# Adding 19 small, unused loads to a tuned softmax

## The chip, the cores and the metric

One core of a Trainium2 chip. The metric is device time in microseconds (us). A transfer is issued when an engine's queue starts it, and has landed when its last byte is reported. DVE is VectorE, ACT is ScalarE, POOL is GpSimd, SP is SyncE. "c0" to "c7" are the eight chunks of the work.

## The reference

```
x: (16, 1024, 512) float32
x_scaled = x / 0.5
exp_x = exp(x_scaled - max(x_scaled, axis=-1))
return exp_x / sum(exp_x, axis=-1)
```

It is a softmax over rows of 512, at temperature 0.5. The kernel reads 33.55 MB and writes 33.55 MB.

## The kernel before

The rows are cut into eight chunks of 128 partitions x 16 rows x 512 (4 MB each) in six buffers; c6 and c7 reuse the buffers of c0 and c1. DVE finds the maxima and multiplies by the reciprocals, ACT takes the exponentials. Loads are issued from Sync's queue. Stores are issued from ACT's queue, in the middle of ACT's own work.

```python
    def load(c):
        if c < BUFS:                                   # BUFS = 6
            chunks[c] = data.tile([P, G, D], fp32, name="xt")
        else:
            chunks[c] = chunks[c - BUFS]
        xt = chunks[c]
        for lo, hi in LOADS[c]:
            nc.sync.dma_start(out=xt[:, lo:hi, :], in_=xr[c][:, lo:hi, :])
    ...
    def store(i):
        ...
                nc.scalar.dma_start(
                    out=outr[c][:, lo:hi, :], in_=chunks[c][:, lo:hi, :]
                )

    shift(0)                         # maxima (DVE); loads the chunk first
    shift(1)
    exponentials(0)                  # ACT
    for i in range(n):
        if i + 1 < n:
            exponentials(i + 1)
        scale_vector(i)              # reciprocal, multiply (DVE)
        scale_scalar(i)              # the last rows of the chunk (ACT)
        if i + 2 < n:
            shift(i + 2)
        store(i)
```

Semaphores are not in this source; the framework deals them out. The built program and the semaphore events of the trace show how: the 17 DMAs issued from Sync and ACT take eight completion semaphores in turn, A to H. A DMA that takes one over is made to wait until the DMA that had it last has landed. The order, with the landing in us in the trace of before:

| semaphore | first use | second use | third use |
|---|---|---|---|
| A | load c0, first part (5.6) | store c1 (88.6) | store c7 (159.7) |
| B | load c0, rest (12.9) | load c6 (95.0) | |
| C | load c1 (22.6) | load c7 (115.0) | |
| D | load c2 (32.3) | store c2 (108.0) | |
| E | load c3 (42.4) | store c3 (121.1) | |
| F | store c0 (69.3) | store c4 (130.7) | |
| G | load c4 (56.3) | store c5 (140.4) | |
| H | load c5 (75.6) | store c6 (150.1) | |

Every second user is due long after its predecessor has landed. The store of c3, for instance, is issued at 92.3 and inherits E from a load that landed at 42.4.

## Time and profile before

The time is 162.5 us (2 runs, 162.26 and 162.73).

| of the 160.6 us span | before |
|---|---|
| DVE busy | 134.6 us |
| ACT busy | 102.1 us |
| DMA moved | 67.13 MB, mean 418 GB/s |
| last store issued, landed | 147.55, 159.71 us |

The page of the kernel before, its busy times and the two lower rows of the 40 slices (a digit is tenths of a slice; DMA is the mean over the 16 DMA engines):

```profile
DVE 134.6 (84%) x45; ACT 102.1 (64%) x273; POOL 0.2 (0%) x4
...
DMA  5999999999999999999999999999999999999993
GB/s 182 471 400 506 400 400 498 408 392 484 424 400 384 400 457 449 400 441 465 400 424 473 408 408 492 400 392 498 416 392 490 424 392 457 457 392 449 465 392 139
```

The DMA engines are full from the second slice to the last but one. The view of waits of the kernel before, with engine and line, what it waited for, us in total, times, longest:

```profile
ACT xt L85 <- DVE bias L78: 41.2, 10, 5.9
DVE negmax L74 <- DMA xt<-in_x_dram: 9.5, 2, 4.8
DVE recip L100 <- ACT xt L85: 1.8, 1, 1.8
```

DVE waits for the first loads and then hardly ever. ACT waits for DVE. So ACT has slack, while DVE and the DMA engines have nearly none. The timeline of the kernel before, around the store of c3 (start, duration, engine, line; in square brackets the engine's idle time before and what ended it; other lines of the same stretch are left out, here and in the timelines below):

```profile
92.27 0.34 ACTq L119 DMA_DIRECT2D out_dram<-xt  x1
96.25 0.72 ACT L85 ACTIVATE xt<-xt,bias 128x512 f32<-128x512 f32 x1 [4.01 <-DVE bias L78]
108.89 0.34 ACTq L119 DMA_DIRECT2D out_dram<-xt  x1
112.74 0.24 DVE L100 RECIPROCAL recip<-sums 128x16 f32<-128x16 f32 x1
```

The store of c3 goes out at 92.27. The exponentials of c5 start at 96.25, when DVE delivers their bias. They end near 107.5, and DVE takes the reciprocal of their sums at 112.74. ACT is thus some 5 us ahead of DVE here.

### The profile page before, as it was taken

How to read it: one execution, taken by the hardware profiler on the slowest of the kernel's cores; microseconds unless marked ns; L12 is line 12 of the kernel's file. 1: busy time of each engine (PE TensorE's matmuls, PEld its weight loads, DVE VectorE, ACT ScalarE, POOL GpSimd, SP SyncE). 2: the span in 40 equal slices, each digit the busy share in tenths (PEclk: the TensorE clock that was granted, in tenths of full speed). 3: DMA queues.
4: the chain of work that ended last, by engine and by line, in shares of the span. 5: the costliest groups of instructions: out<-in, count | busy, mean ns of one | idle time of the engine just before them, and what ended most of it. 6: DMA issues, size and time to landing. Idle time of an engine off the chain costs nothing.

```text
span 160.6 us, 402 instructions
## 1 busy us (share of the span) xinstructions
DVE 134.6 (84%) x45; ACT 102.1 (64%) x273; POOL 0.2 (0%) x4
## 2 busy tenths in 40 slices
DVE  0507999999999999999999999999999999957000
ACT  3071549069979963998199909991899891790000
POOL 0000000000000000000000000000000000000000
DMA  5999999999999999999999999999999999999993
GB/s 182 471 400 506 400 400 498 408 392 484 424 400 384 400 457 449 400 441 465 400 424 473 408 408 492 400 392 498 416 392 490 424 392 457 457 392 449 465 392 139
DMA packets 2450, 67.13 MB, mean 418 GB/s; under 512 B 272, under 2 KB 272, under 8 KB 272
## 3 DMA queue, kind: packets, MB, share of 16 engines
q1 hardware_dynamic: 1296, 33.56, 49.3%
q10 hardware_dynamic: 1152, 33.55, 48.4%
q14 instruction: 2, 0.02, 0.0%
HBM read 33.55 MB, written 33.55 MB: 418 GB/s over the span
## 4 chain that ended last, share of the span: by engine, by line
DVE 80%; DMA 7%; ACT 4%; issue 0%; SPq 0%
DVE negmax L74 42%; DVE xt L102 36%; DMA xt<-in_x_dram 7%; ACT xt L85 4%; DVE bias L78 1%; DVE recip L100 1%; SPq L66 0%
## 5 line engine op out<-in xcount | busy, mean ns | idle before, releaser
L85 ACT ACTIVATE xt<-xt,bias 128x512 f32<-128x512 f32 x128 | 90.4, 708 | 41.7 <-DVE bias L78 41.2
L74 DVE TENSOR_REDUCE negmax<-xt 128x16 f32<-128x8192 f32 (+2 forms) x11 | 69.9, 6352 | 9.5 <-DMA xt<-in_x_dram 9.5
L102 DVE TENSOR_TENSOR xt<-xt,recip 128x7168 f32<-128x7168 f32 (+2 forms) x11 | 62.0, 5637 | 0.4
L85 ACT ACTIVATION_READ_ACCUMULATOR xt<-xt,bias 128x1 f32 x128 | 23.9, 187 | 0.0
L111 ACT ACTIVATE xt<-xt,recip 128x512 f32<-128x512 f32 x15 | 9.9, 706 | 0.0
L100 DVE RECIPROCAL recip<-sums 128x16 f32<-128x16 f32 (+2 forms) x11 | 2.4, 218 | 1.8 <-ACT xt L85 1.8
L78 DVE TENSOR_SCALAR bias<-negmax 128x16 f32<-128x16 f32 (+2 forms) x11 | 1.9, 173 | 0.4
L52 ACT ACT_TABLE_LOAD x1 | 1.3, 1283 | 0.7 <-PEq L148 0.7
L51 DVE MEMSET warm<- 128x1 f32 x1 | 0.1, 59 | 0.8 <-PEq L148 0.8
L52 ACT ACTIVATE warm<-warm 128x1 f32<-128x1 f32 x1 | 0.2, 203 | 0.0
L148 POOL MEMSET const-bfloat16-1.0<- 128x1 bf16 x1 | 0.1, 103 | 0.0
L148 POOL MEMSET const-uint8-127<- 128x1 uint8 x1 | 0.1, 103 | 0.0
L148 POOL MEMSET const-float32-1.0<- 128x1 f32 x1 | 0.1, 100 | 0.0
L148 POOL MEMSET const-float32-0.0<- 128x1 f32 x1 | 0.1, 99 | 0.2 <-issue 0.2
## 6 DMA issues: line engine op xcount, KB each, us to landing
out_dram<-xt ACTq DMA_DIRECT2D x8, 4096.0 KB, 22.8
xt<-in_x_dram SPq DMA_DIRECT2D x7, 4096.0 KB, 30.2
xt<-in_x_dram SPq DMA_DIRECT2D x1, 3072.0 KB, 11.7
xt<-in_x_dram SPq DMA_DIRECT2D x1, 1024.0 KB, 4.9
```

The lines of the kernel that those rows point to most:

```text
L51: nc.vector.memset(warm, 0.0)
L52: nc.scalar.activation(out=warm, in_=warm, func=EXP)
L74: nc.vector.tensor_reduce(negmax[:, 0:b], chunks[c][:, lo:hi, :], axis=AX, op=MAX, negate=True)
L78: nc.vector.tensor_scalar_mul(biases[i][:, 0:b], negmax[:, 0:b], 2.0)
L85: nc.scalar.activation(out=row, in_=row, func=EXP, bias=biases[i][:, g : g + 1], scale=2.0, accum_out=sums[i][:, g : g + 1],)
L100: nc.vector.reciprocal(recips[i][:, 0:b], sums[i][:, 0:b])
L102: nc.vector.tensor_mul(rows, rows, recips[i][:, 0:k].unsqueeze(2).broadcast_to((P, k, D)))
L111: nc.scalar.activation(out=row, in_=row, func=COPY, scale=recips[i][:, g : g + 1])
L148: nc = _bacc.Bacc("TRN2", target_bir_lowering=False, num_devices=1)
```

## The change

The added loads mark points in the program: their sizes are recognisable in the DMA records. Nothing reads what they load. The whole change, with its blank lines left out:

```diff
         xt = chunks[c]
+        if c in (3, 4, 5, 6):
+            mark_pool()
         for lo, hi in LOADS[c]:
             nc.sync.dma_start(out=xt[:, lo:hi, :], in_=xr[c][:, lo:hi, :])
+        if c == 7:
+            mark()
+    junk = stats.tile([16, D], fp32, name="junk", bufs=1)
+    junk2 = stats.tile([16, D], fp32, name="junk2", bufs=1)
+    def mark():
+        for n in range(14, 1, -2):
+            nc.sync.dma_start(
+                out=junk[0:n, 0 : 512 - 4 * n], in_=xr[0][0:n, 0, 0 : 512 - 4 * n]
+            )
+    def mark_pool():
+        for n in (2, 3, 11):
+            nc.gpsimd.dma_start(
+                out=junk2[0:n, 0 : 442 - 4 * n], in_=xr[0][0:n, 0, 0 : 442 - 4 * n]
+            )
```

## The prediction

> **What bounds the kernel now.** The busy table gives DVE 134.6 us (84%) and ACT 102.1 us (64%) of a 160.6 us span. The DMA row reads 9 in every slice but the first and the last: 67.1 MB at a mean of 418 GB/s. The chain of waits starts with the first load (11.7 us), then runs on DVE without a gap from 12.9 to 147.5 us; the last store is issued at 147.6 and lands at 159.7. So DVE and the DMA engines are both nearly full. ACT has slack: it sits idle 41.2 us behind DVE's bias, but every store is issued from ACT's queue, so whatever makes a store wait holds back the exponentials behind it.
>
> **What is added.** 12 loads on GpSimd's queue (4 times 2, 3 and 11 partitions) and 7 on Sync's (14, 12 ... 2 partitions), 120 rows of under 2 KB, together under 0.25 MB. At the measured 309 ns per 8 KB packet, a row costs (estimate) about 0.1 us of one engine: under 1 us per engine in all. Nothing reads them. Each overwrites the one before, so each waits for its landing, but on queues with nothing behind them. By work alone: +0.2 us.
>
> **What I think matters instead.** The trace's semaphore events show that the 17 DMAs from Sync and ACT take eight completion semaphores in turn; the ninth takes the first one's again. The Trainium skill, "DMA: Bandwidth & Descriptors", section "Why a DMA increments its semaphore by 16 and not by 1", says that two DMAs in flight on one semaphore can't be told apart. So I expect each DMA to be made to wait for the one eight places before. Before, that one has always long landed. Seven extra Sync DMAs after the last load use up nearly a whole round of the eight. I assume the order: last load (c7), store of c2, the seven marks, store of c3. Then the store of c3 takes the semaphore of the store of c2, its direct predecessor.
>
> **Cost.** The c2 store is issued at 75.7 and lands at 108.0 (it shares the engines with loads). The c3 store is issued at 92.3 now; it would wait until 108.0, with ACT behind it. The exponentials of c5 now run from 96.2 (bias ready) to 107.5 and would run 108.4 to 119.8. DVE's reciprocal of c5, now at 112.8, would start at 120.0: 7.1 us late. The exponentials of c6 then end at about 132.9, adding 0.6 us. The final store is issued 7.7 us later and lands 7.7 us later (12.1 us alone). The marks themselves land behind the c7 load, from about 115 us on, some 3 us apart, before the stores that reuse their semaphores are due.
>
> **Prediction.** 162.5 + 7.7 + 0.2 = about 170.4 us, 4.9% slower; range 166 to 175. Chances: faster 0.01, same 0.15, slower 0.84.
>
> **What would show it.** Waits of ACT: one hold of about 12 us ahead of the c5 exponentials, ended by the landing of the c2 store; DVE with one new gap of about 7 us near 113 to 120 us; the c3 store issued near 108; one or two DMA slices below 9 near the end; the GpSimd loads landing in a few us each, at no cost.
>
> **What would make it wrong.** If the marks fall elsewhere in the order: all seven before the c2 store makes that store wait for the c7 load, and ACT stops for 26 us (about 181 us); six before the c3 store makes it wait for the c7 load (about 174); marks spread wider leave at most a few us. If the semaphores aren't shared that way, it stays at 162.7. GpSimd's descriptor work could delay DVE or the first load; I give that little weight.

## The result, and the profile after

The time is 169.76 us (2 runs, 169.75 and 169.78), 4.5% slower: the ratio is 1.0447, with a 95% interval of 1.0382 to 1.0512. Ratios here are the record's, over the fast runs of the same rounds, so not quite the ratios of the medians that are quoted. Executions over 1.5% slower than the fastest of the same kernel are left out of the means.

The page of the changed kernel (same rows as before):

```profile
DVE 134.8 (80%) x45; ACT 102.1 (61%) x273; POOL 6.6 (4%) x16
...
DMA  5998999999899999999989899999589388988885
GB/s 189 442 495 374 488 391 468 407 429 435 383 375 485 390 464 414 422 445 399 476 383 495 382 484 390 484 383 417 240 375 503 130 375 374 499 374 375 374 374 250
```

The work of DVE and ACT is the same to 0.2 us. What is new is idle time of the DMA engines in the last third: slices of 240 and 130 GB/s, where every slice before, first and last aside, had at least 384. Its view of waits:

```profile
POOL junk L85 <- DMA junk<-in_x_dram: 76.1, 11, 8.4
ACT xt L106 <- DVE bias L99: 32.5, 8, 5.9
ACT xt L106 <- DMA out_dram<-xt: 16.7, 1, 16.7
DVE recip L121 <- ACT xt L106: 9.9, 3, 7.5
```

ACT has one wait that was not there, 16.7 us, ended by the landing of a store. DVE, which hardly waited for ACT before, now does for 9.9 us. POOL waits 76.1 us for its own loads, one after the other, and nobody waits for POOL. The timeline of the changed kernel at the same place:

```profile
89.38 0.33 SPq L68 DMA_DIRECT2D xt<-in_x_dram  x1
89.75 33.13 SPq L79 DMA_DIRECT2D junk<-in_x_dram  x4
108.58 0.34 ACTq L140 DMA_DIRECT2D out_dram<-xt  x1
109.02 0.72 ACT L106 ACTIVATE xt<-xt,bias 128x512 f32<-128x512 f32 x1 [16.66 <-DMA out_dram<-xt]
120.44 0.25 DVE L121 RECIPROCAL recip<-sums 128x16 f32<-128x16 f32 x1 [7.48 <-ACT xt L106]
121.66 0.34 ACTq L140 DMA_DIRECT2D out_dram<-xt  x1
```

The store of c3 goes out at 108.58 instead of 92.27. By the semaphore events the store of c2 had landed at 108.48. The exponentials of c5 start 12.8 us later than before; DVE's reciprocal of c5, 7.7 us later. The chain of work that ended last, followed back by the profile, now runs through that wait (start, duration, what):

```profile
75.78 32.70 DMA out_dram<-xt
108.58 0.34 ACTq L140
109.02 7.92 ACT xt L106 x23
```

The semaphores in the built program, from the last load on, are now:

| semaphore | was | now |
|---|---|---|
| C | load c7 | load c7 |
| D | store c2 | store c2 |
| E, F, G, H | store c3, c4, c5, c6 | Sync's loads of 14, 12, 10, 8 rows |
| A, B, C | store c7 (A) | Sync's loads of 6, 4, 2 rows |
| D | | **store c3, which has to wait for store c2** |
| E, F, G, H | | store c4, c5, c6, c7 |

### The profile page after: what moved, and what is told of

It is laid out like the page before. It is cut to its first block, busy times and chain, and to the rows that moved or that the text cites. A ratio compares the mean times of both kernels' runs of the same rounds, so it can differ in the third digit from the quotient of the medians.

```text
span 168.0 us, 429 instructions
## 1 busy us (share of the span) xinstructions
DVE 134.8 (80%) x45; ACT 102.1 (61%) x273; POOL 6.6 (4%) x16
## 4 chain that ended last, share of the span: by engine, by line
DVE 40%; DMA 26%; ACT 24%; issue 1%; ACTq 0%; SPq 0%
ACT xt L106 23%; DVE negmax L95 22%; DMA out_dram<-xt 19%; DVE xt L123 16%; DMA xt<-in_x_dram 7%; ACT xt L132 1%; DVE bias L99 1%; DVE recip L121 1%; ACTq L140 0%; SPq L68 0%; ACTq L106 0%
## 5 line engine op out<-in xcount | busy, mean ns | idle before, releaser
L85 POOL DMA_DIRECT2D junk<-in_x_dram x12 | 6.4, 531 | 76.9 <-DMA junk<-in_x_dram 76.1
```

The source lines that it names most:

```text
L85: nc.gpsimd.dma_start(out=junk2[0:n, 0 : 442 - 4 * n], in_=xr[0][0:n, 0, 0 : 442 - 4 * n])
```

## The experiments

The theory: the seven Sync loads take seven of the eight semaphores, so the c3 store takes over that of the store just ahead of it. ACT, which has to issue that store, stops until then, and DVE runs out of exponentials. The rivals: A, the GpSimd loads cost the time; B, the chain of Sync loads that wait for one another does; C, a cost for each load or packet.

Each result gives the median, the range and the kernel before of the same chip and rounds. All kernels computed the right result.

### pool_only: without Sync's loads

```diff
-        if c == 7:
-            mark()
```

> The change without its seven Sync loads; the twelve GpSimd loads stay. Theory (the c3 store is held by the semaphore it shares with the c2 store): the semaphores are dealt as before, the c3 store is issued near 92.3 us, time 162.5 to 162.9 us. Rival A (the GpSimd loads cost the time, by their descriptor work beside DVE or in the DMA engines): most of the 7 us stay, 167 us or more.

Measured: 163.80 us (163.57 to 163.81) against 162.28; ratio 1.0088 (1.0071 to 1.0105). The c3 store was issued at 92.24. DVE is busy for 134.6 us as before and the second part of c0 lands at 12.83 (12.86), so GpSimd's 6.3 us of issuing delays neither. So rival A falls as the main cause. But the GpSimd loads cost 1.4 us (by the ratio) where I expected at most 0.4; the last three runs take that up.

### sync_only: without GpSimd's loads

```diff
-        if c in (3, 4, 5, 6):
-            mark_pool()
```

> The change without its twelve GpSimd loads; the seven Sync loads stay. Theory: all of the loss stays, 169.4 to 169.9 us, the c3 store issued near 108.5 us. Rival A: back to 162.5 to 163 us. Both together: in between.

Measured: 169.33 us (168.98 to 169.78) against 162.28; ratio 1.0435 (1.0413 to 1.0457). The c3 store was issued at 107.86, right after the c2 store landed at 107.76. The time is just below the expected range. The seven Sync loads alone make nearly all of the loss. The two parts do not add up: 7.1 us and 1.4 us alone, 7.3 us together (by the ratios; own_rows, next, has both and shows 7.4 us with a narrower interval).

### own_rows: Sync's loads need not wait for each other

```diff
-    junk = stats.tile([16, D], fp32, name="junk", bufs=1)
+    junk = stats.tile([56, D], fp32, name="junk", bufs=1)
...
-                out=junk[0:n, 0 : 512 - 4 * n], in_=xr[0][0:n, 0, 0 : 512 - 4 * n]
+                out=junk[at : at + n, 0 : 512 - 4 * n],
+                in_=xr[0][0:n, 0, 0 : 512 - 4 * n],
             )
+            at += n
```

> As changed, but each of the seven Sync loads writes partitions of its own, so they need not wait for one another; the order of the semaphores stays. Theory: unchanged at 169.3 to 170 us, the c3 store still issued near 108.5 us. Rival B (the chain of loads that wait for one another stands in the way, on Sync's queue or at the end): faster by several us, towards 163.

Measured: 169.72 us (169.68 to 169.86) against 162.28; ratio 1.0459 (1.0444 to 1.0475). In the change the seven loads land one after the other, from 112.3 to 136.0 us. Here six have landed by 113.4, so that chain is gone (the seventh, at 118.4, had to wait for semaphore C, from the c7 load). The time is the same and the c3 store still goes out at 108.66. Rival B falls.

### hold_c3_only: the wait without any load

```diff
             if hi == end:
+                if c == 3:
+                    nc.scalar.activation(
+                        out=chunks[2][0:1, 0, 0:1], in_=warm[0:1, 0:1], func=COPY
+                    )
                 nc.scalar.dma_start(
```

This is the kernel before. The added instruction writes one element of c2's buffer and so has to wait until the store of c2 has read it and landed. The result stays right, as the store has already gone.

> The kernel before, with no added load at all; ahead of the c3 store ACT writes one element of c2's buffer, which has to wait for the landing of the c2 store. Theory: that hold alone makes the loss, 169.3 to 170.2 us, the c3 store issued near 108.5 us, DVE idle some 7 us ahead of the reciprocal of c5. Rivals A and B, and any cost of small packets in the engines: 162.5 to 163 us.

Measured: 169.28 us (169.16 to 169.33) against 162.28; ratio 1.0429 (1.0414 to 1.0445). The time is 0.02 us under the expected range. Its timeline:

```profile
107.94 0.20 ACT L121 ACTIVATE xt<-warm 1x1 f32<-1x1 f32 x1 [15.75 <-DMA out_dram<-xt]
108.00 0.34 ACTq L124 DMA_DIRECT2D out_dram<-xt  x1
108.44 0.72 ACT L85 ACTIVATE xt<-xt,bias 128x512 f32<-128x512 f32 x1 [0.30 <-issue]
119.86 0.25 DVE L100 RECIPROCAL recip<-sums 128x16 f32<-128x16 f32 x1 [7.08 <-ACT xt L85]
```

This is the pattern of the changed kernel, with no extra load in the program: ACT stops 15.75 us for the c2 store, and DVE then stops 7.08 us for ACT. The hold alone gives 7.0 us, of the 7.1 us that the seven Sync loads cost. The late store's own traffic is not what costs: the last store but one has landed (155.00) before the last is issued (155.41), so nothing queues at the end, and the last is late because DVE was. This is the strongest of the runs.

### sync_marks4, sync_marks5, sync_marks6, sync_marks8: other numbers of loads

If the number of loads decides which landing the c3 store inherits, the cost should jump up and down with it. If each load has a price, it should grow evenly.

```diff
-        for n in range(14, 1, -2):
+        for n in range(14, 7, -2):     # 4; 5 and 6 likewise; 8: range(16, 1, -2)
```

> As changed, with four Sync loads (14 to 8 partitions) instead of seven. By the built program the c3 store now takes over the semaphore of the c1 store (lands at 88.6 us in the trace of before), the c4 store that of the c6 load (95.0), the c5 store that of the c7 load (115.0): all before they are due (92.3, 108.9, 125.5). Theory: 162.5 to 162.9 us. Rival C (a cost that grows with the number of loads, one us each): 166.7 us.

> Five Sync loads. The c3 store takes over the semaphore of the c6 load (lands 95 to 96 us): held 3 to 4 us, inside ACT's wait for the bias of c5 (96.2). The c4 store takes over that of the c7 load (115.0), due at 108.9: held 6 us, of which ACT's slack takes about 4.5. Theory: 163 to 165 us, best guess 164.2. Rival C: 167.7 us.

> Six Sync loads, one fewer than in the change. The c3 store takes over the semaphore of the c7 load, which lands near 112 us without the c3 store's traffic. Theory: slower than with seven loads: the c3 store issued near 112.2 us, 3.6 us later than with seven, time 172.8 to 174 us. Rival C: faster than with seven, 168.7 us.

> Eight Sync loads (one of 16 partitions first). The c3 store takes over the semaphore of the first of these loads, which lands right behind the c7 load, near 112.3 us. Theory: 172.8 to 174.2 us, the c3 store issued near 112.4 us. Rival C: 170.8 us.

| Sync loads | c3 store inherits from | c3 store issued | time, us (range) | before | ratio |
|---|---|---|---|---|---|
| 0 (pool_only) | load c3 | 92.24 | 163.80 (163.57 to 163.81) | 162.28 | 1.0088 |
| 4 | store c1 | 92.42 | 164.13 (164.04 to 164.27) | 162.58 | 1.0108 |
| 5 | load c6 | 96.42 | 164.61 (164.08 to 164.71) | 162.58 | 1.0129 |
| 6 | load c7 | 112.27 | 173.45 (173.36 to 173.59) | 162.58 | 1.0681 |
| 7 (change) | store c2 | 108.58 | 169.76 (169.75 to 169.78) | 162.50 | 1.0447 |
| 8 | first Sync load | 112.51 | 174.04 (173.80 to 174.14) | 162.58 | 1.0715 |

Six loads are 3.7 us slower than seven, and one more than five costs 9 us. Rival C, an even price, falls. The issue times of the c3 store were forecast to half a microsecond. The times with 5, 6 and 8 loads fell into the expected ranges; with 4 the time came out 1.2 us above it, near pool_only: these kernels all carry the GpSimd loads, whose cost I had left out.

Five loads show how much is forgiven. The c3 store waits until 96.42, which ACT would have spent waiting for the bias of c5 anyway. The c4 store waits for the c7 load and goes out at 116.47 instead of 108.89. The view of waits of sync_marks5 shows this second hold and what DVE lost:

```profile
ACT xt L106 <- DMA xt<-in_x_dram: 7.4, 1, 7.4
DVE recip L121 <- ACT xt L106: 4.8, 2, 3.0
```

DVE loses 3.0 us more than before, and the last store is issued 3.2 us later, at 150.75. Yet it lands only 1.2 us later than in pool_only (161.85 against 160.69). When compute is on time the last store queues behind the one ahead of it: in the kernel before it is issued at 147.55 while its predecessor lands at 150.06. A delay of the computation first uses up that queue.

### marks_on_gpsimd: all 19 loads, but from GpSimd

```diff
     def mark():
         for n in range(14, 1, -2):
-            nc.sync.dma_start(
+            nc.gpsimd.dma_start(
```

> All nineteen loads stay, with their sizes, places and the waits among themselves; the seven of Sync are issued from GpSimd's queue instead, which by the built program has semaphores of its own. Theory: the stores' semaphores are dealt as before, the c3 store is issued near 92.3 us, 162.5 to 163.0 us. Rival (the loads' work or packets cost the time, whoever issues them): 169 to 170 us.

Measured: 164.48 us (164.41 to 164.66) against 162.36; ratio 1.0130 (1.0113 to 1.0147). The c3 store was issued at 92.24. The same loads of the same sizes, issued where they take none of the stores' semaphores, cost 2.1 us instead of 7.3. The semaphores were forecast correctly, but the time was 1.5 us too low, again for the small loads' own cost.

### pool_4x16, pool_12x16, pool_12x1: what the small loads cost by themselves

In pool_only every instruction of DVE and ACT is where it was: the last store is issued at 147.52 (before 147.55). But its last engine finishes at 160.69 instead of 159.71, and its first at 158.77 instead of 158.49. After that, Sync goes through eight waits, some 60 ns each by the trace, before its drain instruction. Call what comes after the last landing the close: to the drain it takes 0.51 us, where before it took 0.12. So the 1.4 us are about 1.0 us in the DMA engines and 0.5 us at the close. The number of semaphores is not what sets this: in the runs with twelve GpSimd loads Sync waits for A to H in this order, and only what stands from the last store's semaphore on is left after its landing. That takes 0.51 us where the last store has A (0 and 8 Sync loads), 0.26 with E (4), 0.20 with F (5), 0.14 with G (6) and 0.08 with H (7, the change). In the kernel before the last store has A too, but there the wait for A stands second to last. The question was how the 1.0 us comes about. All three edits change the GpSimd loads of pool_only alone:

```diff
-        for n in (2, 3, 11):           # pool_4x16: for n in (11,):
-                out=junk2[0:n, 0 : 442 - 4 * n], in_=xr[0][0:n, 0, 0 : 442 - 4 * n]
+                out=junk2[0:16, 0 : 442 - 4 * n],      # pool_4x16 and pool_12x16
+                in_=xr[0][0:16, 0, 0 : 442 - 4 * n],   # pool_12x1: 0:1 in both
```

> What the twelve GpSimd loads cost: alone they cost 1.4 us where 0.2 was predicted (163.8 us; the last store lands 1.0 us later, its first engine only 0.3 us later). Here each trio of 2, 3 and 11 rows is one load of 16 rows of 1592 B: the same 64 rows in 4 loads, one row of each for every engine. Theory D (one engine carries a row of every load, 12 times about 70 ns, and the engines have no slack): 4 rows per engine, 0.3 us, plus 0.4 us at the close: 162.9 to 163.1 us, the last store's landings spread as before (1.2 us). Theory E (a cost per load on every engine): a third of 1.4 us: 162.8 us.

> Twelve GpSimd loads of 16 rows each: 12 rows on every engine, three times the rows of the change. Theory D: 12 rows per engine are what the fullest engine of the change carries, so the same time as the change's GpSimd loads alone, 163.7 to 163.9 us, but with a spread of the last store's landings near 1.2 us instead of 1.9, its first landing near 159.4. Rival F (the bytes count): three times the excess, 165 us or more.

> Twelve GpSimd loads of one row each. Theory D with every load starting on the same engine: that engine carries 12 rows, 163.5 to 163.8 us, spread 1.9 us. Theory D with the loads dealt around the engines: one row each, 162.7 to 162.9 us. Theory E (a cost per load, on all engines): 163.5 to 163.8 us with both the first and the last landing of the last store late by 0.9 us or more.

| run | rows per engine, mean | time, us (range) | ratio to before (162.32; pool_only 162.28) | mean landing of the last store, later than before |
|---|---|---|---|---|
| pool_only | 4 | 163.80 (163.57 to 163.81) | 1.0088 | 0.48 us |
| pool_4x16 | 4 | 163.31 (163.03 to 163.64) | 1.0062 | 0.64 us |
| pool_12x16 | 12 | 165.14 (164.78 to 165.24) | 1.0170 | 2.18 us |
| pool_12x1 | 0.75, in pieces | 163.19 (162.80 to 163.59) | 1.0060 | 0.15 us |

The last column is the mean over the 16 engines' semaphore events of the last store in the profiled run. It grows with the rows, so the bytes (or rows) count, as rival F had it: pool_12x16 was expected at 163.7 to 163.9 and took 165.14. The other two missed as well: pool_4x16 was expected at 163.1 at most, and pool_12x1 fell between the ranges of its theories. From 4 to 12 rows the mean landing moves by 2.18 - 0.64 = 1.54 us, or 0.19 us per row (of one trace each: the slowest run of pool_4x16 and the fastest of pool_12x16). The packet records show 67 to 75 ns for such a row. My theory D took those 70 ns for the cost, and so it was off by a factor of more than two. Its other half is supported: in pool_only the landings of the last store are 1.9 us apart (1.2 before), and 2, 3 and 11 rows can only fall on some engines; with 16 rows in each load they are 1.1 us apart (the records do not name the engines). With 4x16 they are 1.55 us apart, more than the 1.2 that I expected, so balance is not all of it. In these two runs the second part of c0 also lands later (13.48 and 13.61 us; before 12.86), and DVE starts that much later; but the last store still queues behind its predecessor, so that is not what its landing shows. Theory E falls: pool_only and pool_12x16 have the same number of loads and differ by 1.3 us.

pool_12x1 did not test what it was made for, though with twelve loads and a delay of 0.15 us it too leaves little room for a cost per load. Its rows were not moved whole: the records show 124-byte, 172-byte and 796-byte packets. The Trainium skill, "DMA: Bandwidth & Descriptors", section "Why a DMA increments its semaphore by 16 and not by 1", has the rule: the largest number of engines up to 16 that divides the count, once software has split a single row. 434 = 14 x 31 floats, 430 = 10 x 43, 398 = 2 x 199 fit it exactly. In time it still cost 1.0 us by the ratio, while its profiled run, at 162.80, was its fastest.

All the packet records together come close to the delays. Summed over the loads, the stores and GpSimd's queue, and divided by 16 engines, they exceed those of the kernel before by 0.64 us in pool_only, 0.75 in pool_4x16, 2.29 in pool_12x16 and 0.24 in pool_12x1, each within 0.2 us of the delay in the table. Of the 2.29 us only 0.99 are GpSimd's own packets; 1.22 are the chunks' 32 KB load packets, which took 1250 ns in the mean where they took 1228. So by these records (one trace each) the rest of a small row's cost lies in load packets that are longer with the small loads beside them.

What stays open is why they are, and what else pool_12x1 pays for in its slower runs.

No run beat the kernel before, and none of these points to a version that could: its DMA engines are full from the second slice on.

## Why the prediction was right

The forecast was 170.4 us, with a range of 166 to 175, and the result 169.76. Point by point:

- **The bound.** "DVE and the DMA engines are both nearly full", with slack on ACT, held, though one stretch of the chain that the prediction gave to DVE, 137.6 to 143.3, is ACT's. hold_c3_only shows the slack: 15.75 us of hold on ACT cost DVE 7.08 us.
- **The mechanism.** "Each DMA to be made to wait for the one eight places before" and the assumed order were right, as the built program, the issue times of nine kernels and the jump between five, six and seven loads show. The Trainium skill page only gave the reason to expect a wait; it says that two DMAs in flight on one semaphore can't be told apart. That reason is not tested here, only the wait.
- **The hold.** Forecast to end at 108.0, measured 108.5. The view of waits shows 16.7 us instead of the "about 12 us" in the prediction, since it puts the whole idle time down to what ended it; 4.0 us of it was ACT's old wait for the bias. The Sync loads landed from 112.3 us on, 1.3 to 7.1 us apart instead of "some 3 us", and still no store had to wait for one.
- **DVE.** Forecast 7.1 us late at the reciprocal of c5, measured 7.7 (120.44 against 112.74).
- **The last store.** Forecast 7.7 us later in issue and in landing. It was issued 8.4 us later (155.99) and landed 7.4 us later (167.10). The term "12.1 us alone" was mis-sized: without a store ahead of it the last store took 11.1 us. The two errors partly cancelled, which was luck.
- **The loads' work.** "+0.2 us" was too low as a price for the loads, and "the GpSimd loads landing in a few us each, at no cost" was wrong. Alone they cost 1.4 us, and all 19 on GpSimd's queue 2.1 us. I had added up the small packets' own records and spread them over the engines, although the engines had no slack: a small row costs more of an engine than its record says, and the last engine to finish counts. In the change itself only 0.4 us of it appears (169.76 against 169.33 without them; the difference is not clear of the spread of sync_only). Part of the reason is the close: in the change the last store has H, and Sync is at its drain 0.08 us after the landing (0.51 in pool_only), so the 0.4 us of these waits are not paid. For the rest a likely reason, argued and not shown apart, is that the hold leaves the DMA engines idle in the last third, where late engines catch up: the last store's landings are 0.17 us apart (1.9 in pool_only). What remains of the loads' work shows at the c2 store, which lands at 108.48 against 107.76 in sync_only (one trace each, that of sync_only its fastest run).
- **The idle DMA slices.** "One or two DMA slices below 9 near the end" was too few: ten of the last twelve are below 9.

## What to carry to other kernels

An added DMA can cost far more than its bytes if completion semaphores are dealt in turn: it changes which earlier transfer each later one has to wait for. After adding any DMA, look which landing each store now inherits; a store issued from a computing engine stops that engine too. Where the DMA engines are full to the end, small transfers are not free either: their own packet records gave less than half of the price here (0.99 of 2.29 us in pool_12x16), so test it. And when two versions differ by some tenths of a us, look at the close as well.

## What the Trainium skill lacked or had wrong

- "DMA: Bandwidth & Descriptors", section "Why a DMA increments its semaphore by 16 and not by 1", warns of two DMAs in flight on one semaphore but does not say what it costs when the wait that prevents it lands on a busy queue: here 7.0 us of 162.3 for one wait (hold_c3_only).
- The same page, "Specifications", gives 512 B as the least transfer for line rate. In pool_12x16 the records of rows of 1592 to 1736 B come near that (67 to 73 ns in the median; at the rate of the 32 KB packets, 1213 ns, 1.7 KB would take 0.06 us), but each row put off the last store by about 0.19 us of an engine. The section does not speak of what small transfers do to the packets beside them.
- The same page, section "Anatomy of one DMA — SWDGE (gpsimd) path", has about 2.0 us fixed per DMA and gives no figure beside other streams. Beside full load and store streams the GpSimd loads of at most 17 KB landed 5.3 to 10.4 us after issue (median 7.1).
- No page that I read says that the final waits for DMA semaphores come one after the other in a fixed order, so that the close depends on which semaphore the last store has: 0.51 us from its landing to Sync's drain in pool_only, 0.08 us in the change, with the same number of semaphores.
